# The mixer's values as one block of 1024 columns, with 7 products for three pairs

## The chip, the cores and the metric

The kernel runs on one core of a Trainium2 chip. The metric is the device time of one execution in microseconds (us). Five engines work side by side, each with its own queue of instructions in a fixed order, and wait for each other by semaphores: TensorE (PE in the profile, its weight loads PEld), VectorE (DVE), ScalarE (ACT), GpSimd (POOL) and SyncE (SP), which issues the transfers. TensorE reads its operands from SBUF and adds into PSUM.

## The reference

One layer of a streaming encoder over 256 frames of 2048 channels in f32: a SwiGLU feed-forward half step, a mixer, cross attention over 256 memory tokens, and a second feed-forward half step. Only the mixer is touched:

```python
h = rms_norm(x, mix_norm)
proj = h @ w_in                        # 2048 x 4112
u, q, k, v, g, a_lr = split(proj, [1024, 1536, 2048, 3072, 4096])
y_pool = pool_mixer(u, pool_w, pool_scale)     # 4 groups of 256 channels, a 256x256 map each
y_gla = gla_mixer(q, k, v, g, a_lr, ...)       # 4 heads, chunks of 64 frames
x = x + concat(y_pool, y_gla) @ w_out
```

So the columns of `w_in` are, in order, 1024 for the pool, 512 queries, 512 keys, 1024 values, 1024 gate and 16 for the decay. A head has 128 query and key columns and 256 value columns. In a head, decayed scores of queries and keys (zero above the chunk's end) weigh the values; the result is normed over its 256 channels, scaled by the norm's gain and multiplied by silu of the gate.

## The kernel before, in words

**Precision by splitting.** Each f32 operand of a large product is split into a high and a low half in a reduced format (fp32r), and three products stand for one: high by high, high by low, low by high. ScalarE casts the high half of a weight (`wh`, line 273), VectorE subtracts to get the low half (`wl`, line 274). The activations are kept split in `xs` and `ys`, tiles of 16 blocks of 128 channels, each with a high and a low half of 256 frames.

**The stream.** The class `Stream` holds the whole kernel as a list of units and operations. A unit is 1 MB of weights (2048 f32 on each of 128 partitions): a transfer into one of three `raw` buffers, a split into one of three `wh`/`wl` buffers, and the products on TensorE. `unit` appends one; `op(f, after)` appends other work behind the `after`th unit from there. On emission the splits run two units ahead of the products (`AHEAD = 2`), and the transfer of unit u + 3 is issued behind the split of unit u. The weight splits are held in their order on ScalarE and VectorE (`in_turn`), and `among_weights` puts other work at a place between them. Beyond that the framework's scheduler sets the order on each engine, by its own estimate of when things are ready. PSUM is a pool of four tiles of two banks each (`ptile`).

**Three forms of a product block.** `block_a` turns the product around (columns on partitions, 512 columns in 4 units of 32 matmuls). `block_b` has frames on partitions, 512 columns and 4 units of 24 matmuls into one PSUM tile. `block_s` has frames on partitions and 1024 columns, in 8 units of 2 channel blocks; a unit has 24 matmuls (`unit_p`), or, where it is listed as a pair in a `Sums` object, 7 products of half size by Strassen's scheme, 21 matmuls (`unit_s` and `seven`). Such a pair needs combinations of its four weight quarters (`split_seven`: T by three additions on line 457, then the split of T and of three of the quarters, `xh`/`xl`), combinations of the activations (`Sums.make`, lines 418 to 430, with a split), two more PSUM tiles (`open_parts`), and at the end additions that put the products together (`combine` and `join`, lines 542 to 557).

**The mixer.** In this order: two `block_a` for the pool's channels, whose evictions (`ev_pool`) write the pool's differences to `ys` blocks 8 to 15; the decay's 16 columns; `block_a` for queries and for keys; the pool's grouped product `pool_unit` from a unit of its own (`load_pool`), whose results `pool_out` writes to `ys` blocks 0 to 7 (lines 230 and 234); two `block_b` for the values, 512 columns each, evicted by ScalarE (`ev_v`) into the tile `v`; two `block_a` for the gate; then the output block. Among the units stand the heads' steps: `scores` scales the queries (lines 1102 and 1104), multiplies with the keys and copies the result to the one score tile `ST` (line 1118); `attend` multiplies `ST` and `v` (lines 1125 and 1128), squares on ScalarE (line 1134) and copies on VectorE (line 1136); `head_squares` adds (line 1140); `head_norms` sums over channels on TensorE (line 1147) and makes the root's reciprocal (lines 206 to 222) for two heads; `head_scale` spreads it (line 227) and scales. `ev_g` evicts a gate tile (lines 312, 313, 317), takes silu, multiplies, and splits into `ys` blocks 8 to 15.

The units of the values hold heads 0 and 1 in part: `scores(0)` comes after the first unit of the second values block, and the rest among its units and the first four gate units.

Of the kernel before, what the change touches and what calls it, by code (L numbers as in the profile page):

```python
# [7 lines left out]
F32 = mybir.dt.float32  # L8
F32R = mybir.dt.float32r
# [5 lines left out]
P = 128  # L15
# [78 lines left out]
def build(ctx, tc, I, out):  # L94
# [36 lines left out]
    def ptile(name):  # L131
        return psum.tile([P, 2, NB], F32, tag="ps", name=name)
# [6 lines left out]
    def uid(s):  # L139
        cnt[0] += 1  # L140
        return f"{s}{cnt[0]}"
# [256 lines left out]
    class Sums:  # L398
# [1 line left out]

        def __init__(self, name, act, pairs, over, room):
            self.name, self.act, self.pairs, self.over = name, act, pairs, over
            self.room, self.where = room, {}

        def make(self, g):
            act, i = self.act, self.pairs.index(g)
            n = 3 if self.over else 4
            if i == 0 or i >= self.room:  # L410
                room, tag = (self.room, self.name) if i == 0 else (1, f"{self.name}{i}")
                t = scope["pool"].tile([P, room * 6 * P], F32R, tag=tag, name=uid(tag))
                held = min(len(self.pairs), self.room) if i == 0 else 1
                t = t[:, : held * 2 * n * P].rearrange("p (g a n s) -> p g a n s", a=2, n=n, s=P)
                self.where.update({i + k: t[:, k] for k in range(held)})
            own = self.where[i]
            a, k = jtile(), slice(2 * g, 2 * g + 2)
            nc.vector.tensor_tensor(
                out=a.rearrange("p (k s) -> p k s", k=2), in0=f32(act[:, k, 0, :]),
                in1=f32(act[:, k, 1, :]), op=ALU.add,  # L420
            )

            a = a.rearrange("p (n s) -> p n s", n=4)
            p11, p21, p12, p22 = (a[:, m] for m in range(4))
            nc.vector.tensor_tensor(out=p11, in0=p11, in1=p21, op=ALU.subtract)
            nc.vector.tensor_tensor(out=p21, in0=p22, in1=p21, op=ALU.subtract)
            nc.vector.scalar_tensor_tensor(
                out=p22, in0=p11, scalar=-1.0, in1=p22, op0=ALU.mult, op1=ALU.subtract
            )
            added = nc.vector.tensor_tensor(out=p12, in0=p12, in1=p22, op=ALU.add)  # L430
            split(own[:, 0], own[:, 1], a[:, 4 - n :])
            if self.over:
                split(act[:, 2 * g, 0, P:], act[:, 2 * g, 1, P:], p11)
            return None, added
# [46 lines left out]
                    banks[n], x, w, start=n in fresh and j == 0, stop=n in ends and j == 2  # L481
                )

    def block_s(srcs, act, sums, order, evict, merge=None, sevens=None, late=0):

# [49 lines left out]

        def combine():

            e = held["e"] = scope["pool"].tile([P, 4, NB], F32, tag="sg", name=uid("sg"), bufs=2)  # L540
            a, b = held["parts"]
            nc.scalar.copy(e[:, 0], a[:, 0])
            nc.vector.tensor_tensor(out=e[:, 3], in0=a[:, 1], in1=e[:, 0], op=ALU.add)
            nc.vector.tensor_tensor(
                out=e[:, 1:3], in0=b, in1=e[:, 3:4].to_broadcast([P, 2, NB]), op=ALU.add
            )
            last = nc.vector.tensor_tensor(out=e[:, 3], in0=b[:, 1], in1=e[:, 1], op=ALU.add)
            if merge is not None:
                merge(e[:, 2:4], e[:, 0:2])
            return None, last  # L550
# [17 lines left out]
                st.unit(srcs[g], unit_p(g))  # L568
        for j in (1, 0):
            st.op(lambda j=j: join(j))  # L570

    def block_b(srcs, act, evict, delay=0):

        n_k = 4 * len(srcs)
        held = {}

        def unit(gi):
            def fn(wh, wl):
                if gi == 0:
                    held["ps"] = ptile(uid("pb"))  # L580
                wh, wl = (w.rearrange("p (k n) -> p k n", n=NB) for w in (wh, wl))
                for kk in range(4):
                    k = 4 * gi + kk
                    for h in range(2):
                        products(held["ps"][:, h, :], act, k, h, wh[:, kk], wl[:, kk],
                                 k == 0, k == n_k - 1)
            return fn

        for gi, src in enumerate(srcs):
            st.unit(src, unit(gi))  # L590
        st.op(lambda: evict(held["ps"]), delay)

    def wload(dst, w, k0, n, n0, cols=NB):
        nc.sync.dma_start(
# [301 lines left out]
    def down_first(wd, k0, nk, last, way):  # L896
# [3 lines left out]

    ffn(I["ffn1_w_gate"][0], I["ffn1_w_up"][0], I["ffn1_w_down"][0], down_first,
        amid_first)
    st.op(close_scope, 1)
    st.op(open_scope("s_mix"), 1)


    w_in = I["w_in"][0]
    mix = {}

    def mt(name, shape, tag=None, bufs=1):  # L910
        t = whole_lines(scope["pool"], shape, F32, tag or name, uid(name), bufs)
        mix[name] = t
        return t
# [149 lines left out]
    def ev_k(p, ps):  # L1063
# [3 lines left out]
        joined(ps, k)  # L1067
        nc.vector.tensor_tensor(out=k, in0=k, in1=mix["e"][:, 2 * p : 2 * p + 2, :], op=ALU.mult)

    block_a(wblock(w_in, 0), xs, ev_pool(0))  # L1070
    block_a(wblock(w_in, NB), xs, ev_pool(1))
    st.unit(load_a, a_unit, split_a)
    st.op(ev_a)
    st.op(decay, 2)
    block_a(wblock(w_in, 2 * NB), xs, ev_q)
    block_a(wblock(w_in, 3 * NB), xs, ev_k)
    st.unit(load_pool, pool_unit)
    for g in range(4):
        st.op(lambda g=g: pool_out(g))

    def ev_v(b):
        def evict(ps):
            if b == 0:
                mt("v", [P, 2, 2 * NB])
                s = mt("ST", [P, 2, S])
                nc.gpsimd.memset(s[64:128, 0, 0:CH], 0.0)
                nc.gpsimd.memset(s[64:128, 1, 2 * CH : 3 * CH], 0.0)
            for h in range(2):
                nc.scalar.activation(
                    mix["v"][:, h, b * NB : (b + 1) * NB], ps[:, h, :], AF.Copy, scale=Rcol[:, h : h + 1]  # L1090
                )
        return evict

    def scores(h):
        q, kd, E, F = mix["q"][:, h, :], mix["k"][:, h, :], mix["E"], mix["F"]
# [22 lines left out]
            nc.vector.tensor_copy(s[part, j // 2, j * CH :], ps[part, j // 2, j * CH : S])  # L1118

    def attend(h):  # L1120
        s, v = mix["ST"], mix["v"]
        po = ptile(uid("po"))
        for vt in range(2):
            col = h * DV + vt * P
            nc.tensor.matmul(
                po[:, vt, :S], v[:, 0, col : col + P], s[:, 0, :], start=True, stop=False
            )
            nc.tensor.matmul(
                po[:, vt, 2 * CH : S], v[:, 1, col : col + P], s[:, 1, 2 * CH :], start=False, stop=True
            )  # L1130
        if h % 2 == 0:
            mix["oz", h // 2] = as_four(m4())
        q = mix["osq", h] = ttile()
        nc.scalar.activation(q, po[:, :, :S], AF.Square)
        i = h % 2
        nc.vector.tensor_copy(mix["oz", h // 2][:, 2 * i : 2 * i + 2, :], po[:, :, :S])

    def head_squares(h):
        sq = mix["osq", h]
        nc.vector.tensor_tensor(out=sq[:, 0, :], in0=sq[:, 0, :], in1=sq[:, 1, :], op=ALU.add)  # L1140
# [14 lines left out]
    def head_scale(b):  # L1155
        ps = ptile(uid("ps"))
        for i in range(4):
            spread(ps[:, i // 2, :], i % 2, mix["diag"][i])
        for i in range(2):
            oz = mix["oz", b][:, 2 * i : 2 * i + 2, :]  # L1160
            nc.vector.tensor_tensor(out=oz, in0=oz, in1=bc(ps[:, i, :S]), op=ALU.mult)

    def ev_g(b):
# [10 lines left out]
            split_pair(ys, 8 + 2 * h, t)  # L1174
        return evict

    for b in range(2):
        block_b(wblock(w_in, (4 + b) * NB), xs, ev_v(b))
        for i in range(2):
            h = 2 * b + i  # L1180
            at = 1 + i - b
            st.op(lambda h=h: scores(h), at)
            st.op(lambda h=h: attend(h), at + 1)
            st.op(lambda h=h: head_squares(h), at + 1)
        st.op(lambda b=b: head_norms(b), 5 - 2 * b)
        st.op(lambda b=b: head_scale(b), 6 - b)
    block_a(wblock(w_in, 6 * NB), xs, ev_g(0), (0, 0))
    block_a(wblock(w_in, 7 * NB), xs, ev_g(1))
    st.op(close_scope, 1)
# [377 lines left out]
```

## Time and profile before

| | us |
|---|---|
| median of 3 runs | 2088.07 |
| lowest and highest | 2087.95, 2088.35 |
| the profiled execution | 2089.16 |
| its span, first to last instruction | 2087.4 |

| engine | busy us | share of the span |
|---|---|---|
| TensorE | 2074.1 | 99% |
| weight loads | 1728.9 | 83% |
| VectorE | 1791.1 | 86% |
| ScalarE | 1129.9 | 54% |
| POOL | 13.1 | 1% |

A row of a group gives line, engine, operation, what it writes and reads, shape and count, then busy time and mean duration of one in ns, then the idle time of the engine ahead of these instructions and what ended it. A row of the timeline gives start, duration, engine, line and operation. Matmuls are pipelined, so the mean duration of one (some 390 ns) is more than the distance from one to the next; the distance is read from a stretch's length and its count.

### The profile page before, as it was taken

How to read it: one execution, taken by the hardware profiler on the slowest of the kernel's cores; microseconds unless marked ns; L12 is line 12 of the kernel's file. 1: busy time of each engine (PE TensorE's matmuls, PEld its weight loads, DVE VectorE, ACT ScalarE, POOL GpSimd, SP SyncE). 2: the span in 40 equal slices, each digit the busy share in tenths (PEclk: the TensorE clock that was granted, in tenths of full speed). 3: DMA queues.
4: the chain of work that ended last, by engine and by line, in shares of the span. 5: the costliest groups of instructions: out<-in, count | busy, mean ns of one | idle time of the engine just before them, and what ended most of it. 6: DMA issues, size and time to landing. Idle time of an engine off the chain costs nothing.

```text
span 2087.4 us, 24205 instructions
## 1 busy us (share of the span) xinstructions
PE 2074.1 (99%) x9672; PEld 1728.9 (83%) x9672; DVE 1791.1 (86%) x1635; ACT 1129.9 (54%) x1116; POOL 13.1 (1%) x41
## 2 busy tenths in 40 slices
PE   9999999999999999999999999999999999999998
PEld 7888888888888888888888888888888888888886
DVE  7999899988998677678789777879998999989974
ACT  7655455644654545455755444556554555545544
POOL 0000000000000000000000000000000000000001
PEclk9999999999999999999999999999999999999999
DMA  7556666566656755457655455666576665676673
GB/s 263 202 196 228 241 222 205 191 230 223 237 191 238 240 166 183 160 187 266 230 183 183 160 182 181 213 211 205 178 242 216 237 209 184 226 239 222 209 255 118
DMA packets 131321, 435.94 MB, mean 209 GB/s; under 512 B 9860, under 2 KB 13544, under 8 KB 130824
## 3 DMA queue, kind: packets, MB, share of 16 engines
q1 hardware_dynamic: 131176, 434.38, 61.5%
q8 instruction: 76, 1.25, 0.2%
q14 instruction: 37, 0.30, 0.0%
q10 hardware_dynamic: 32, 0.01, 0.0%
HBM read 417.58 MB, written 16.78 MB: 208 GB/s over the span
## 4 chain that ended last, share of the span: by engine, by line
PE 96%; DVE 2%; issue 1%; ACT 0%; DMA 0%; SPq 0%; DVEq 0%
PE pt L356 55%; PE pt L480 25%; PE pa L341 6%; PE pe L356 3%; PE pb L356 2%; PE ph L747 1%; PE pl L1283 1%; PE pv L1322 1%; PE px L758 1%; DVE wl L461 0%; DVE T L457 0%; DVE xl L274 0%; DVE wl L274 0%; DMA x<-in_x 0%; PE pp L976 0%
## 5 line engine op out<-in xcount | busy, mean ns | idle before, releaser
L274 DVE TENSOR_TENSOR wl<-raw,wh 128x2048 fp32r<-128x2048 f32 (+2 forms) x268 | 600.5, 2248 | 166.4 <-ACT wh L273 165.6
L356 PE MATMUL pt<-wh,xs 128*128 128x512 f32 x2128 | 681.7, 390 | 0.5 <-ACT xs L230 0.5
L273 ACT CAST wh<-raw 128x2048 fp32r<-128x2048 f32 (+2 forms) x268 | 502.9, 1880 | 315.0 <-PE pt L356 136.8
L356 PEld LDWEIGHTS pt<-wh,xs 128*128 128x128 f32 x2128 | 398.3, 188 | 82.2 <-ACT xs L230 0.7
L460 ACT CAST wh<-T 128x1024 fp32r<-128x1024 f32 x228 | 239.8, 1054 | 364.2 <-DVE T L457 355.2
L356 PE MATMUL pt<-wh,ys 128*128 128x512 f32 x1360 | 428.3, 390 | 0.0
L356 PE MATMUL pt<-wl,xs 128*128 128x512 f32 x1064 | 415.6, 391 | 0.0
L356 PEld LDWEIGHTS pt<-wh,ys 128*128 128x128 f32 x1360 | 254.9, 188 | 52.5
L356 PE MATMUL pt<-wl,ys 128*128 128x512 f32 x680 | 264.9, 390 | 0.0
L461 DVE TENSOR_TENSOR wl<-T,wh 128x2048 fp32r<-128x2048 f32 x114 | 260.4, 2284 | 1.2 <-ACT wh L460 0.5
L356 PEld LDWEIGHTS pt<-wl,xs 128*128 128x128 f32 x1064 | 199.8, 188 | 41.2 <-DVE wl L274 0.2
L274 DVE TENSOR_TENSOR xl<-raw,xh 128x1536 fp32r<-128x1536 f32 x114 | 199.7, 1752 | 19.2 <-ACT xh L273 19.2
L273 ACT CAST xh<-raw 128x1536 fp32r<-128x1536 f32 x114 | 168.7, 1480 | 43.9 <-PE pt L480 28.7
L457 DVE TENSOR_TENSOR T<-T,raw 128x512 f32<-128x512 f32 x228 | 157.4, 690 | 6.1
L356 PEld LDWEIGHTS pt<-wl,ys 128*128 128x128 f32 x680 | 127.7, 188 | 26.3
L480 PE MATMUL pt<-wh,xs 128*128 128x512 f32 x364 | 141.8, 390 | 0.0
L457 DVE TENSOR_TENSOR T<-raw 128x1024 f32<-128x1024 f32 x114 | 138.9, 1219 | 1.6 <-DMA raw<-in_ffn_w_gate 1.1
L480 PE MATMUL pt<-xh,xs 128*128 128x512 f32 x364 | 136.7, 391 | 0.1
L341 PE MATMUL pa<-xs,wh 128*128 128x512 f32 x384 | 135.6, 397 | 0.0
L480 PE MATMUL pt<-wh,xe 128*128 128x512 f32 x320 | 124.5, 389 | 0.0
L341 PE MATMUL pa<-xs,wl 128*128 128x256 f32 x384 | 106.8, 282 | 0.0
L341 PEld LDWEIGHTS pa<-xs,wh 128*128 128x128 f32 x384 | 71.7, 188 | 16.4 <-issue 0.3
(238 smaller groups left out, 2286.2 us busy)
## 6 DMA issues: line engine op xcount, KB each, us to landing
raw<-in_ffn_w_down SPq DMA_DIRECT2D x88, 1024.0 KB, 5.5
raw<-in_ffn_w_up SPq DMA_DIRECT2D x80, 1024.0 KB, 5.0
raw<-in_ffn_w_gate SPq DMA_DIRECT2D x77, 1024.0 KB, 5.1
raw<-in_w_in SPq DMA_DIRECT2D x32, 1024.0 KB, 5.2
raw<-in_xattn_w_kv SPq DMA_DIRECT2D x32, 1024.0 KB, 5.1
raw<-in_w_out SPq DMA_DIRECT2D x16, 1024.0 KB, 5.5
raw<-in_xattn_w_q SPq DMA_DIRECT2D x16, 1024.0 KB, 5.6
raw<-in_xattn_w_o SPq DMA_DIRECT2D x16, 1024.0 KB, 5.5
```

The source lines that it names most:

```text
L273: in_turn("scalar", lambda: nc.scalar.copy(hi, src))
L274: in_turn("vector", lambda: nc.vector.tensor_tensor(out=lo, in0=src, in1=f32(hi), op=ALU.subtract))
L341: nc.tensor.matmul(o, w, x, start=k == 0 and i == 0, stop=last and i == 1)
L356: nc.tensor.matmul(ps, a, w, start=first and i == 0, stop=last and i == 2)
L457: in_turn("vector", lambda: nc.vector.tensor_tensor(out=o, in0=a, in1=b, op=ALU.add))
L460: in_turn("scalar", lambda: nc.scalar.copy(th[:, c], t[:, c]))
L461: in_turn("vector", lambda: nc.vector.tensor_tensor(out=tl, in0=t, in1=f32(th), op=ALU.subtract))
L480: nc.tensor.matmul(banks[n], x, w, start=n in fresh and j == 0, stop=n in ends and j == 2)
L747: nc.tensor.transpose(v[:, i, h * P : (h + 1) * P], g[:, h, i * P : (i + 1) * P], ident)
L758: nc.tensor.transpose(v[:, j, h * P : (h + 1) * P], x[:, h, j * P : (j + 1) * P], ident)
L1283: nc.tensor.matmul(ps[:, t, :M], ys[:, 4 * h + d, a, tok], xa["K", h][:, d, b, :], start=i == 0, stop=i == 11,)
L1322: nc.tensor.matmul(ps[:, d, :S], xa["V", h][:, m, a, col], xa["PT", h][:, m, b, :], start=i == 0, stop=i == 5,)
```

## The change

- The values become one `block_s` of 1024 columns. Pairs 1, 4 and 6 of its 8 units are done with 7 products; the combinations of the activations are kept in `ys` blocks 8 to 15 (`place`), free once the pooled product has read them. The mixer's scope gets single buffers for `T`, `xh` and `xl` (`MIX_HOMES`), and the tile `v` becomes two tiles' worth of a four-part tile that holds the joined products (`v_tile`). `ev_v` now scales in place, a head pair at a time.
- `block_b` is gone.
- The pool's grouped product stands ahead of the keys' block, not behind it.
- The sums of the activations are made one per unit, from the first key unit on.
- `scores(0)` is listed behind the sixth unit from the values' start; the heads follow the values, one per unit; `head_norms` and `head_scale` come 3 and 4 units, and 6 and 7 units, behind the values.
- The score tile `ST` shares the place of the decay's weights, and its zeros are written before the keys.

```diff
-        def __init__(self, name, act, pairs, over, room):
+        def __init__(self, name, act, pairs, over, room, place=None):
             self.name, self.act, self.pairs, self.over = name, act, pairs, over
-            self.room, self.where = room, {}
+            self.room, self.where, self.place = room, {}, place
...
-                t = scope["pool"].tile([P, room * 6 * P], F32R, tag=tag, name=uid(tag))
+                if self.place is not None:
+                    t = self.place
+                else:
+                    t = scope["pool"].tile([P, room * 6 * P], F32R, tag=tag, name=uid(tag))
...
-            e = held["e"] = scope["pool"].tile([P, 4, NB], F32, tag="sg", name=uid("sg"), bufs=2)
+            e = held["e"] = home()
...
+    MIX_HOMES = {"xh": [("xh", 3 * NB, 1)], "xl": [("xl", 3 * NB, 1)]}
     st.op(close_scope, 1)
-    st.op(open_scope("s_mix"), 1)
+    st.op(open_scope("s_mix", MIX_HOMES), 1)
...
+    V_PAIRS, V_ORDER = (1, 4, 6), (0, 1, 2, 3, 4, 5, 6, 7)
...
+    def score_tile():
+        t = mt("ST", [P, 2, S], tag="wa2")
+        nc.gpsimd.memset(t[64:128, 0, 0:CH], 0.0)
+        nc.gpsimd.memset(t[64:128, 1, 2 * CH : 3 * CH], 0.0)
+
+    def v_tile():
+        return scope["pool"].tile([P, 4, NB], F32, tag="v", name=uid("v"))
+
+    def ev_v(j, c):
+
+        mix["v", j] = c
+        for t in range(2):
+            nc.scalar.activation(c[:, t, :], c[:, t, :], AF.Copy, scale=Rcol[:, t : t + 1])
...
     block_a(wblock(w_in, 2 * NB), xs, ev_q)
-    block_a(wblock(w_in, 3 * NB), xs, ev_k)
     st.unit(load_pool, pool_unit)
     for g in range(4):
         st.op(lambda g=g: pool_out(g))
...
+    v_sums = Sums("", xs, V_PAIRS, False, len(V_PAIRS), ys[:, 8:].rearrange("p k a s -> p (k a s)"))
+    st.op(score_tile, 1)
+    for i, g in enumerate(V_PAIRS):
+        st.op(lambda g=g: among_weights(lambda: v_sums.make(g)), 1 + i)
+    block_a(wblock(w_in, 3 * NB), xs, ev_k)
...
-        s, v = mix["ST"], mix["v"]
+        s, v = mix["ST"], mix["v", h // 2]
...
-            col = h * DV + vt * P
+            col = h % 2 * DV + vt * P
...
+    st.op(lambda: scores(0), 6)
+    block_s(wwide(w_in, 4 * NB), xs, v_sums, V_ORDER, ev_v, home=v_tile)
+    for h in range(H):
+        st.op(lambda h=h: attend(h), 1 + h)
+        st.op(lambda h=h: head_squares(h), 1 + h)
+        if h + 1 < H:
+            st.op(lambda h=h: scores(h + 1), 1 + h)
     for b in range(2):
-        block_b(wblock(w_in, (4 + b) * NB), xs, ev_v(b))
-        for i in range(2):
-            h = 2 * b + i
-            at = 1 + i - b
-            st.op(lambda h=h: scores(h), at)
-            st.op(lambda h=h: attend(h), at + 1)
-            st.op(lambda h=h: head_squares(h), at + 1)
-        st.op(lambda b=b: head_norms(b), 5 - 2 * b)
-        st.op(lambda b=b: head_scale(b), 6 - b)
+        st.op(lambda b=b: head_norms(b), 3 + 3 * b)
+        st.op(lambda b=b: head_scale(b), 4 + 3 * b)
     block_a(wblock(w_in, 6 * NB), xs, ev_g(0), (0, 0))
```

More of the change, by code (lines that the diff above doesn't have):

```diff
@@ L482, in seven, with parts_tile, block_s @@
                 )
-    def block_s(srcs, act, sums, order, evict, merge=None, sevens=None, late=0):
+    def parts_tile():
+        return scope["pool"].tile([P, 4, NB], F32, tag="sg", name=uid("sg"), bufs=2)
+    def block_s(srcs, act, sums, order, evict, merge=None, sevens=None, late=0, home=parts_tile):
         sevens = [g for g in order if g in (sevens or sums.pairs)]
@@ L570, in block_s @@
             st.op(lambda j=j: join(j))
[L572 to L591, printed above, removed]
     def wload(dst, w, k0, n, n0, cols=NB):
@@ L1079, in build @@
         st.op(lambda g=g: pool_out(g))
[L1081 to L1092, printed above, removed]
+    v_sums = Sums("", xs, V_PAIRS, False, len(V_PAIRS), ys[:, 8:].rearrange("p k a s -> p (k a s)"))
[3 more added lines that the diff above has]
+    block_a(wblock(w_in, 3 * NB), xs, ev_k)
     def scores(h):
```

## The prediction

> **What bounds the kernel now.** I read the page first, then the sums by stretch of time around the mixer, then groups by form, then the timelines of VectorE and ScalarE. From the page, parts 1 and 4:
>
> ```profile
> span 2087.4 us, 24205 instructions
> PE 2074.1 (99%) x9672; PEld 1728.9 (83%) x9672; DVE 1791.1 (86%) x1635; ACT 1129.9 (54%) x1116; POOL 13.1 (1%) x41
> PE 96%; DVE 2%; issue 1%; ACT 0%; DMA 0%; SPq 0%; DVEq 0%
> ```
>
> TensorE is the path: a matmul less is time gained, and any microsecond in which TensorE waits is lost. The stretches that the change touches (values, then heads and gate; below them the values alone, the keys and the pooled product by their tiles). Columns: stretch, its length, busy time and instructions of TensorE, its weight loads, VectorE, ScalarE and POOL (an engine with none is left out), then the granted clock:
>
> ```profile
> 812.63:861.87 49.24, 49.24 (x235) 39.93 (x233) 27.21 (x38) 22.61 (x27) 0.00 (x0) 1.00 0.58 189
> 861.87:913.91 52.04, 52.04 (x316) 45.82 (x314) 35.56 (x60) 24.41 (x26) 0.00 (x0) 1.00 0.44 145
> ```
> ```profile
> 812.63:839.95 27.32, 27.32 (x120) 22.34 (x120) 1.27 (x2) 1.00 0.59 191
> ```
> ```profile
> 784.38:806.89 22.51, 22.51 (x129) 19.42 (x127) 1.37 (x2) 1.65 (x3) 1.00 0.54 182
> ```
> ```profile
> 806.89:812.63 5.74, 5.74 (x48) 5.69 (x47) 0.47 (x1) 0.47 (x1) 1.00 0.62 210
> ```
>
> The first two columns are equal in every row: TensorE is never idle here. A values matmul takes 27.32 / 120 = 0.228, one of the keys or the gate 22.51 / 128 = 0.176 (a wide and a narrow one alternate). VectorE is at 27.21 of 49.24 in the values; its idle time before the weight splits of this whole stretch is
>
> ```profile
> L274 DVE TENSOR_TENSOR wl<-raw,wh 128x2048 fp32r<-128x2048 f32 x16 | 36.7, 2291 | 28.1 <-ACT wh L273 28.0
> ```
>
> **Matmuls removed.** The values go from 2 x 4 units of 24 products (192) to 5 units of 24 and 3 pairs of 7 x 3 (183). 9 x 0.228 = 2.05 gained, all on the path. That is the whole possible gain: 0.1%, while about 0.2% (4.2 us) is what a measurement of this kernel can tell from no change.
>
> **The pooled product ahead of the keys.** Its 48 matmuls and the keys' 128 are the same in either order (28.25 together), so the values again start 28.25 after the queries' end (784.38), at 812.63. Its load moves past four key loads on SP's queue, and each of these goes one place later:
>
> ```profile
> raw<-in_w_in SPq DMA_DIRECT2D x32, 1024.0 KB, 5.2
> raw<-in_pool_w SPq DMA_DIRECT2D x1, 1024.0 KB, 5.4
> ```
>
> Equal sizes, 5.2 to 5.4 to land, three buffers ahead: taken at nothing, covered by the two units (over 11 us) between a load and its use; without that cover it would be some 5. The two memsets of the score tile move back on POOL, 1% busy: nothing. The eight evictions of the pooled product (a ScalarE and a VectorE half each) now fall into the keys; that matters below.
>
> **VectorE's new work and where it queues.** A unit with 7 products needs, beside the same splits, these:
>
> ```profile
> L461 DVE TENSOR_TENSOR wl<-T,wh 128x2048 fp32r<-128x2048 f32 x114 | 260.4, 2284 | 1.2 <-ACT wh L460 0.5
> L274 DVE TENSOR_TENSOR xl<-raw,xh 128x1536 fp32r<-128x1536 f32 x114 | 199.7, 1752 | 19.2 <-ACT xh L273 19.2
> L457 DVE TENSOR_TENSOR T<-T,raw 128x512 f32<-128x512 f32 x228 | 157.4, 690 | 6.1
> L457 DVE TENSOR_TENSOR T<-raw 128x1024 f32<-128x1024 f32 x114 | 138.9, 1219 | 1.6 <-DMA raw<-in_ffn_w_gate 1.1
> ```
>
> so 1.22 + 2 x 0.69 + 1.75 + 2.28 = 6.63 of VectorE against 2.29 of a plain unit, while TensorE needs only 21 x 0.228 = 4.8. Ahead of it come three sums of the activations (L418 to L430 and a split of 512 columns, nearest row PT's), and the evictions of pool and keys:
>
> ```profile
> L418 DVE TENSOR_TENSOR j<-xs 128x512 f32<-128x512 f32 x12 | 8.2, 682 | 0.0
> L425 DVE TENSOR_TENSOR j<-j 128x128 f32<-128x128 f32 x25 | 7.2, 289 | 0.6
> L280 DVE TENSOR_TENSOR PT<-pt,PT 128x512 fp32r<-128x512 f32 x4 | 2.6, 683 | 0.0
> L234 DVE SCALAR_TENSOR_TENSOR ys<-pp,gains,ys 128x256 fp32r<-128x256 f32 x8 | 3.7, 480 | 0.7 <-ACT ys L230 0.7
> L313 DVE TENSOR_TENSOR k<-pa,c 128x512 f32<-128x512 f32 x2 | 1.4, 688 | 1.4 <-ACT c L312 1.4
> ```
>
> A sum is 0.68 + 4 x 0.29 + 0.68 = 2.52, three 7.6. With 3 x 4.3 more for the pairs and 5.0 for recombining (five additions of T's sizes: 2 x 0.69 + 3 x 1.22), VectorE gets 25.6 more, nearly the 28.1 that it has idle. The question is where. Up to here VectorE's queue of the two kernels has the same times, in the stretch after the queries:
>
> ```profile
> 793.52 0.69 DVE L313 TENSOR_TENSOR q<-pa,c 128x512 f32<-128x512 f32 x1
> 794.76 0.68 DVE L1059 SCALAR_TENSOR_TENSOR q<-q,R 128x512 f32<-128x512 f32 x1
> 795.37 2.38 DVE L1052 TENSOR_TENSOR F<-F,E 128x4 f32<-128x4 f32 x1
> 797.66 2.28 DVE L274 TENSOR_TENSOR wl<-raw,wh 128x2048 fp32r<-128x2048 f32 x1
> ```
> ```profile
> 794.91 2.81 POOL L1045 TENSOR_TENSOR m<-m,R 128x1024 f32<-128x1024 f32 x1 [32.37 <-ACT m L1044]
> ```
>
> The changed kernel's order of instructions on VectorE puts, from 797.66 to the low half that the first pair's second product reads (xl of the second values unit): three plain splits (6.84), three scalings of q (0.75), six pool evictions (2.88), the three sums (7.56), T (2.60), four instructions on the keys (2.76), xl (1.75): 25.1. (The keys' second PSUM tile is the queries': its join above ends at 794.2, and TensorE's order touches that tile after 30 key products, at 784.38 + 5.74 + 30 x 0.176 = 795.4: no wait.) Neighbours overlap by 0.09 (795.37 + 2.38 against 797.66) where the next does not read the last, at about 24 of 38 places: -2.1. Twice it waits for ScalarE, which in turn waits for a VectorE half of the pool's evictions (the cast of the last key unit now stands behind one): about +1.0. So xl is ready at 821.7. TensorE wants it 28 matmuls after the values' start: 812.63 + 28 x 0.228 = 819.0. **It waits 2.7**, and 0.1 more for the low half of T behind it: 2.8. If all 38 overlap and no ScalarE wait occurs, 0.4; with no overlap, 4.8. I take 2.8, worked from the order as it stands. After that VectorE is ahead again (two plain splits against two units of 5.5), and the later pairs, whose single xh and xl buffers come free after the first 9 products, have over 2 to spare.
>
> [...]
>
> **The heads behind the values.** Four heads now lie between the gate's first four units, one per unit, where before two lay in the values. The matmuls are the same, but their order on TensorE is not: after the last product of the fourth gate unit (call it G) come, with no gate product between them, attend of head 2, scores of head 3, the norms of heads 0 and 1, attend of head 3, the spread of these norms, and only then gate unit five, whose PSUM tile is free only when VectorE has joined the first gate tile. VectorE and ScalarE rows of before for these steps, and the TensorE time of scores, attend, half a norm, spread, with VectorE's copies of a score tile last:
>
> ```profile
> 877.06:877.85 0.79, 0.79 (x9) 0.59 (x9) 0.43 (x1) 0.32 (x1) 0.00 (x0) 1.00 0.00 0
> 884.41:885.72 1.31, 1.31 (x10) 1.20 (x8) 0.86 (x1) 0.42 (x1) 0.00 (x0) 1.00 0.04 13
> 885.72:886.08 0.36, 0.36 (x6) 0.36 (x5) 0.36 (x1) 0.16 (x1) 0.00 (x0) 1.00 0.00 0
> 878.66:879.47 0.81, 0.81 (x10) 0.81 (x8) 0.81 (x1) 0.00 (x0) 0.00 (x0) 1.00 0.00 0
> 857.79:859.18 1.39, 1.39 (x6) 1.11 (x7) 1.29 (x4) 0.00 (x0) 0.00 (x0) 1.00 0.31 41
> ```
> ```profile
> 871.89 0.69 DVE L1136 COPY m<-po 128x512 f32<-128x512 f32 x1
> 872.49 0.42 DVE L1140 TENSOR_TENSOR t<-t 128x256 f32<-128x256 f32 x1
> 872.83 0.25 DVE L1104 TENSOR_SCALAR m<-q,E 128x64 f32<-128x64 f32 x1
> ...
> 873.64 0.25 DVE L1104 TENSOR_SCALAR m<-q,E 128x64 f32<-128x64 f32 x1
> 873.83 0.18 DVE L210 RECIPROCAL r<-chain 128x4 f32<-128x4 f32 x1
> ...
> 874.65 0.88 DVE L222 TENSOR_SCALAR diag<-ident,r 128x128 f32<-128x128 f32 x4
> ```
> ```profile
> 889.65 1.29 ACT L312 COPY c<-pa 128x512 f32<-128x512 f32 x2 [3.14 <-PE pa L341]
> 890.84 1.91 ACT L273 CAST wh<-raw 128x2048 fp32r<-128x2048 f32 x1
> 892.76 1.28 ACT L1168 ACT_TABLE_LOAD   x1
> ```
> ```profile
> L1134 ACT ACTIVATE t<-po 128x512 f32<-128x512 f32 x4 | 2.4, 599 | 2.8 <-PE po L1128 2.8
> ```
>
> From G: ScalarE copies the second gate half (0.6), casts gate unit seven (1.91, ahead in its queue), then squares head 2 (0.60): G + 3.1. VectorE copies head 2 and sums (0.69 + 0.42), then scales q for head 3 (six, 872.83 to 873.89, 1.06): the first three by G + 4.7, all by G + 5.1. TensorE's scores of head 3 begin, two norm halves (0.72), the rest of the scores: G + 6.2. On VectorE the root's reciprocal comes ahead of the score copies: G + 6.4, copies (1.39) G + 7.8. Attend of head 3 ends G + 8.6; the norm's factors (from the end of L210 at 874.01 to the last diagonal at 875.53, 1.5) are done at G + 9.3, the spread G + 9.6, the join (0.69) G + 10.0. TensorE's own work in it is 1.31 + 0.79 + 0.72 + 1.31 + 0.81 = 4.9, **so 5.1 of waiting**. Without the cast in the way it is 3.1 (the cast takes 1.9); with the table load, here hidden under VectorE's scalings, exposed and a second 0.6 copy behind G, 6.9. I take 5.1. Behind it gate units five to eight (22.5) cover both gate evictions and the last norms, and the output block's own waits stay as they are.
>
> **Sum.** -2.05 + 2.8 + 5.1 = +5.8. The profiled execution, 2089.16 against the median of 2088.07, goes to 2095.0; the median to 2093.9.
>
> **Rivals.**
> - First pair hidden, heads not: VectorE overlaps more than I count, its lower end being 0.4. Price -2.05 + 5.1 = +3.0: 2091.1. Against it: 25 us of queue in the 21.3 between 797.66 and 819.0.
> - Heads hidden, first pair not: 2088.07 - 2.05 + 2.8 = 2088.8. Against it: no gate product stands in that part of TensorE's order.
> - Nothing waits: only the 9 matmuls count, 2086.0, not slower. It decides if the xl of the first pair is in place by 819.0 and head 2's square does not wait for the cast. For it: before, the same kinds of chain were covered without loss (both stretches above are full).
> - Both at their upper ends: -2.05 + 4.8 + 6.9 = +9.7: 2097.7.
> [...]
>
> **How the numbers follow.** Forecast 0.48, first pair hidden 0.15, heads hidden 0.08, nothing waits 0.12, both at the upper end 0.10, clock 0.07. The prediction is the forecast's 2093.9, whose own range (first pair 1.5 to 4, heads 4 to 6) is 2091.5 to 2096. From 2088.5 to 2098 only "nothing waits" and small tails are out. Slower by over 0.2% (above 2092.2): 0.48 + 0.10 + 0.07 = 0.65; within: 0.15 + 0.08 + 0.10 = 0.33; faster 0.02, the tail of "nothing waits".
>
> **What will show it.** Right: a TensorE gap of about 3 before an L480 product with xl some 6 after the values begin, ended by VectorE xl L274; a run of waits of about 5 among scores, attend and norms after the fourth gate unit, ended by ScalarE and VectorE of the heads; 183 values products. Wrong: either stretch with TensorE's columns equal, a granted clock under 1.00 there, or a wait in the output block that before did not have.

## The result, and the profile after

The changed kernel takes 2098.72 us (median of 4 runs; 2097.56 to 2100.69); the kernel before, run beside it, 2088.21 (2087.95 to 2088.63). The ratio is 1.005, 95% interval 1.0038 to 1.0062: slower by 10.5 us, where 5.8 was forecast. The profiled execution takes 2098.07. From its page, the span, the busy times and the chain of work that ended last:

```profile
span 2096.3 us, 24240 instructions
PE 2077.4 (99%) x9663; PEld 1731.5 (83%) x9663; DVE 1814.3 (87%) x1670; ACT 1137.1 (54%) x1126; POOL 12.6 (1%) x41
PE 94%; DVE 4%; ACT 1%; issue 1%; DMA 0%; SPq 0%; DVEq 0%
```

TensorE has its 9 matmuls less (9663 against 9672) and is still busy for 3.3 us more, and VectorE has 4% of the chain where it had 2%. The sums by stretch of time place it (columns as in the prediction: length, TensorE, its weight loads, VectorE, ScalarE, POOL, then the granted clock, which is the share of TensorE's full clock). The rows are the values up to the first scores, the gate up to G (the end of gate unit four, here 886.12), the heads' chain behind G up to gate unit five (898.55), and, without their first 4.4 us, the other four gate units:

```profile
811.90:857.78 45.88, 43.21 (x184) 35.06 (x182) 40.42 (x36) 22.11 (x18) 0.00 (x0) 0.96 0.62 206
857.78:886.12 28.34, 28.34 (x171) 24.17 (x170) 18.74 (x34) 12.66 (x17) 0.00 (x0) 1.00 0.53 172
886.12:898.55 12.43, 8.13 (x41) 6.84 (x40) 6.40 (x24) 5.47 (x10) 0.00 (x0) 0.77 0.09 34
902.95:923.44 20.49, 20.49 (x124) 18.03 (x123) 15.37 (x21) 8.92 (x9) 0.00 (x0) 1.00 0.51 164
```

Before, the values and the gate were full and at clock 1.00. Now the values have 2.67 idle and a clock of 0.96, the chain 4.30 idle and a clock of 0.77; the other two rows are full and at 1.00. From the start of the values to the end of the gate it is 111.54 (811.90 to 923.44) against 101.28 before (812.63 to 913.91), 10.3 more, where the whole span grew by 8.9: the loss lies here, whole. The 9 matmuls should have made it 99.2, so 12.3 were added, of which idle time is only 6.97.

TensorE's timeline in the two places (start, duration, then in brackets the idle time ahead and what ended it):

```profile
821.10 0.80 PE L483 MATMUL pt<-xl,xs 128*128 128x512 f32 x1 [2.67 <-DVE xl L274]
821.69 0.63 PE L483 MATMUL pt<-xh,xs 128*128 128x512 f32 x1
822.12 0.63 PE L483 MATMUL pt<-wh,ys 128*128 128x512 f32 x1
...
890.89 0.62 PE L1106 MATMUL pq<-m,k 128*64 128x256 f32 x2 [3.31 <-DVE m L1098]
...
894.29 1.19 PE L1119 MATMUL po<-ST,v 128*128 128x256 f32 x2 [0.99 <-DVE ST L1112]
```

Both waits are where the prediction put them, ended by what it named. The rows behind the first show the part that was missed: the matmuls start 0.43 apart (821.69, 822.12), not 0.228. The sums by stretch again, cut at the borders at which the granted clock changes; they lie on a grid of 3.413 us (from 821.03 to 892.71 it is 71.68, 21 times that):

```profile
817.62:821.03 3.41, 0.81 (x4) 0.34 (x2) 3.41 (x5) 1.62 (x2) 0.00 (x0) 1.00 0.00 0
821.03:824.44 3.41, 3.34 (x8) 2.67 (x9) 3.41 (x3) 3.03 (x2) 0.00 (x0) 0.50 0.64 187
...
885.88:889.29 3.41, 1.71 (x11) 1.37 (x9) 0.06 (x1) 3.30 (x6) 0.00 (x0) 1.00 0.36 144
889.29:892.71 3.42, 1.82 (x14) 1.43 (x15) 2.11 (x9) 1.61 (x4) 0.00 (x0) 1.00 0.00 0
892.71:896.12 3.41, 2.42 (x11) 1.91 (x8) 2.73 (x12) 0.20 (x1) 0.00 (x0) 0.50 0.02 5
896.12:899.53 3.41, 3.41 (x15) 3.21 (x14) 2.48 (x6) 0.60 (x1) 0.00 (x0) 0.50 0.00 0
```

Three stretches of 3.41 us have the clock at 0.50, one behind the first wait and two behind the heads'. In them TensorE is busy for 3.34 + 2.42 + 3.41 = 9.17 us, half of which, 4.6, full clock would have saved. With the 6.97 idle that is 11.6 of the 12.3; 0.7 is not placed.

### The profile page after: what moved, and what is told of

It is laid out like the page before. It is cut to its first block, busy times and chain, and to the rows that moved or that the text cites. A ratio compares the mean times of both kernels' runs of the same rounds, so it can differ in the third digit from the quotient of the medians.

```text
span 2096.3 us, 24240 instructions
## 1 busy us (share of the span) xinstructions
PE 2077.4 (99%) x9663; PEld 1731.5 (83%) x9663; DVE 1814.3 (87%) x1670; ACT 1137.1 (54%) x1126; POOL 12.6 (1%) x41
## 4 chain that ended last, share of the span: by engine, by line
PE 94%; DVE 4%; ACT 1%; issue 1%; DMA 0%; SPq 0%; DVEq 0%
PE pt L356 56%; PE pt L483 26%; PE pa L341 5%; PE pe L356 3%; PE ph L733 1%; DVE wl L274 1%; DVE T L460 1%; PE pl L1277 1%; PE pv L1316 1%; PE px L744 0%; DVE xl L274 0%; DVE wl L464 0%; ACT wh L273 0%; DMA x<-in_x 0%; PE pq L1106 0%
## 5 line engine op out<-in xcount | busy, mean ns | idle before, releaser
L274 DVE TENSOR_TENSOR wl<-raw,wh 128x2048 fp32r<-128x2048 f32 (+2 forms) x265 | 593.7, 2247 | 152.4 <-ACT wh L273 151.6
L356 PE MATMUL pt<-wh,xs 128*128 128x512 f32 x2208 | 707.3, 390 | 0.1
L273 ACT CAST wh<-raw 128x2048 fp32r<-128x2048 f32 (+2 forms) x265 | 497.0, 1880 | 305.5 <-PE pt L356 134.4
L356 PEld LDWEIGHTS pt<-wh,xs 128*128 128x128 f32 x2208 | 413.3, 188 | 85.0 <-ACT xs L230 0.4
L463 ACT CAST wh<-T 128x1024 fp32r<-128x1024 f32 x234 | 245.9, 1053 | 367.0 <-DVE T L460 360.6
L356 PE MATMUL pt<-wl,xs 128*128 128x512 f32 x1104 | 431.2, 391 | 0.0
L464 DVE TENSOR_TENSOR wl<-T,wh 128x2048 fp32r<-128x2048 f32 x117 | 267.3, 2284 | 1.3 <-ACT wh L463 0.5
L356 PEld LDWEIGHTS pt<-wl,xs 128*128 128x128 f32 x1104 | 207.3, 188 | 42.8
L274 DVE TENSOR_TENSOR xl<-raw,xh 128x1536 fp32r<-128x1536 f32 x117 | 204.9, 1751 | 21.3 <-ACT xh L273 21.3
L483 PE MATMUL pt<-wh,xs 128*128 128x512 f32 x370 | 144.2, 390 | 0.0
L483 PE MATMUL pt<-xh,xs 128*128 128x512 f32 x376 | 141.5, 392 | 0.1
```

The source lines that it names most:

```text
L273: in_turn("scalar", lambda: nc.scalar.copy(hi, src))
L274: in_turn("vector", lambda: nc.vector.tensor_tensor(out=lo, in0=src, in1=f32(hi), op=ALU.subtract))
L463: in_turn("scalar", lambda: nc.scalar.copy(th[:, c], t[:, c]))
L464: in_turn("vector", lambda: nc.vector.tensor_tensor(out=tl, in0=t, in1=f32(th), op=ALU.subtract))
L483: nc.tensor.matmul(banks[n], x, w, start=n in fresh and j == 0, stop=n in ends and j == 2)
```

## The experiments

The question was whether the half clock is an effect of the two waits, and whether the terms 2.8 and 5.1 are right without it. Each kernel is the changed kernel with the edit shown, except where another is named. The kernel before ran beside each group: 2088.01 beside the first four, 2088.33 beside the second four, 2088.24 beside the last two.

**The first pair one unit later.**

```diff
-    V_PAIRS, V_ORDER = (1, 4, 6), (0, 1, 2, 3, 4, 5, 6, 7)
+    V_PAIRS, V_ORDER = (2, 4, 6), (0, 1, 2, 3, 4, 5, 6, 7)
```

> The 7-product pairs are 2, 4 and 6 instead of 1, 4 and 6; nothing else. Theory of waits with the clock: the first pair comes one unit of 24 products (5.5 us) later, VectorE has its xl ready in time, so both the 2.8 us wait in the values and the half clock behind it (1.5 us) go: 4.3 less than the changed kernel's 2098.7, about 2094.4, with a granted clock of 1.00 over all the values. Rival, waits alone (the clock has another cause than the wait): the wait goes and the half clock stays, about 2095.9. Rival, VectorE is short over the whole block and not only ahead of the first pair: the wait only moves, 2098.7. The heads behind the fourth gate unit still take some 12.4 us.

Measured: 2093.62 (2093.14 to 2095.11), ratio 1.0027 (1.0017 to 1.0038): 5.1 less than the changed kernel. Sums by stretch of this kernel: the values, then a part of its heads' chain:

```profile
811.90:853.40 41.50, 41.50 (x185) 34.08 (x183) 39.67 (x35) 20.38 (x17) 0.00 (x0) 1.00 0.68 228
...
884.02:887.43 3.41, 1.30 (x9) 0.94 (x9) 2.00 (x8) 2.13 (x5) 0.00 (x0) 1.00 0.00 0
887.43:890.85 3.42, 2.43 (x11) 1.96 (x11) 1.84 (x8) 0.20 (x1) 0.00 (x0) 0.50 0.00 0
```

In the values both the idle time and the half clock are gone; VectorE, busy for 39.67 of 41.50, is nearly full there and yet late nowhere. It was short ahead of the first pair only. It remains 5.6 over before, so with the 2.05 saved some 7.7 are the heads', whose chain has its half clock as it was (887.43 to 894.26).

**The heads one unit earlier.** Then this with the pairs 2, 4 and 6 together.

```diff
-    for h in range(H):
-        st.op(lambda h=h: attend(h), 1 + h)
-        st.op(lambda h=h: head_squares(h), 1 + h)
+    for h, at in enumerate((0, 1, 2, 3)):
+        st.op(lambda h=h: attend(h), at)
+        st.op(lambda h=h: head_squares(h), at)
         if h + 1 < H:
-            st.op(lambda h=h: scores(h + 1), 1 + h)
+            st.op(lambda h=h: scores(h + 1), at)
     for b in range(2):
-        st.op(lambda b=b: head_norms(b), 3 + 3 * b)
-        st.op(lambda b=b: head_scale(b), 4 + 3 * b)
+        st.op(lambda b=b: head_norms(b), (2, 5)[b])
+        st.op(lambda b=b: head_scale(b), (3, 6)[b])
```

> Each head is one unit earlier (head h at 0 + h units behind the values, the norms at 2 and 5, the factors at 3 and 6), so that gate products stand between most of the heads' steps on TensorE; the values with the pairs 1, 4 and 6 are left as they are. Theory of waits with the clock: the heads' 7.5 us (5.0 of waits, 2.5 of half clock) go, less up to 2 us for the first attend, which now comes straight behind the values: 2091.2 to 2093.2, with the half clock only in the values. Rival, waits alone: 5.1 go, 2093.6 to 2095.6, and a clock under 1.00 stays around the heads. Rival, the heads' chain is too long for any place among the gate units: the waits come back in other places, 2096 or more.

> Both edits together: pairs 2, 4 and 6, and the heads one unit earlier. Theory of waits with the clock: the values cost -2.05 (9 matmuls) and nothing else, the heads up to 2 us for the first attend, a granted clock of 1.00 throughout: 2086.1 to 2088.2, not slower than before. Rival, waits alone: what of the clock is not tied to the two waits stays, some 2.7 us more: 2088.9 to 2090.9.

Measured: 2100.23 (ratio 1.0058, 1.0043 to 1.0073) and 2093.68 (1.0026, 1.0016 to 1.0037). Neither came as expected; the second was to be no slower than before. TensorE's waits longer than 1 us from the first attend on, in the first kernel and then in the second:

```profile
863.23 1.19 PE L1119 MATMUL po<-ST,v 128*128 128x256 f32 x2 [3.93 <-ACT v L1070]
868.46 0.62 PE L1106 MATMUL pq<-m,k 128*64 128x256 f32 x2 [2.32 <-DVE m L1098]
```
```profile
857.48 0.67 PE L1119 MATMUL po<-ST,v 128*128 128x256 f32 x2 [3.09 <-ACT v L1070]
862.33 1.08 PE L1106 MATMUL pq<-m,k 128*64 128x256 f32 x2 [2.33 <-DVE m L1098]
```

The chain behind G no longer waits, but the first attend stands straight behind the last values product and waits 3.1 to 3.9 for ScalarE to scale `v`, and the next scores 2.3 for VectorE, with half clock behind both (862.88 to 866.29 and 869.70 to 873.12 in the first kernel, 858.25 to 868.49 in the second). I had allowed 2 for this. The rival that the waits only change place was right for this edit.

**The clock alone: idle work in the two waits.** Transposes of the identity into PSUM columns that are overwritten or never read: 12 behind the first product of the values' first pair, 15 ahead of head 3's scores.

```diff
-    def seven(banks, act, sums, g, fresh, ends, weights, order):
+    def seven(banks, act, sums, g, fresh, ends, weights, order, fill=0):
...
+                if n == "P1" and j == 0:
+                    for _ in range(fill):
+                        nc.tensor.transpose(banks["P6"][:, :P], ident, ident)
...
-                seven(held["banks"], act, sums, g, fresh, ends, weights, order)
+                seven(held["banks"], act, sums, g, fresh, ends, weights, order,
+                      fill if g == sevens[0] else 0)
...
         ps = ptile(uid("pq"))
+        for _ in range(15 if h == 3 else 0):
+            nc.tensor.transpose(ps[:, 0, S : S + P], ident, ident)
...
-    block_s(wwide(w_in, 4 * NB), xs, v_sums, V_ORDER, ev_v, home=v_tile)
+    block_s(wwide(w_in, 4 * NB), xs, v_sums, V_ORDER, ev_v, home=v_tile, fill=12)
```

> The changed kernel with idle work for TensorE in its two longest waits: 12 transposes of the identity (0.21 us each, 2.5 in all) behind the first product of the first pair, and 15 (3.2 us) ahead of head 3's scores, into PSUM columns that are overwritten or never read. No wait is taken away. Theory of waits with the clock: the granted clock stays at 1.00 in both places, the first products behind each wait take 0.228 and not 0.427 us: 1.5 less in the values and some 2.5 less in the heads, about 2094.7. Rival (the half clock comes with the load, not with standing still): the clock falls all the same and the time is 2098.7 or some tenths more, for transposes that run longer than the wait.

Measured: 2093.99 (2093.13 to 2095.24), ratio 1.0028 (1.0018 to 1.0038): 4.7 less than the changed kernel, with 27 matmuls more. TensorE's timeline in the values, then the sums by stretch behind the first wait and of the heads' chain:

```profile
819.07 1.47 PE L488 MATMUL pt<-ident 128*128 128x128 f32 x12
...
822.08 0.50 PE L483 MATMUL pt<-xl,xs 128*128 128x512 f32 x1 [1.30 <-DVE xl L274]
```
```profile
821.50:828.00 6.50, 5.92 (x25) 4.67 (x26) 6.50 (x4) 4.48 (x3) 0.00 (x0) 1.00 0.57 173
886.00:896.20 10.20, 8.28 (x60) 7.26 (x59) 6.64 (x25) 5.35 (x9) 0.00 (x0) 1.00 0.08 31
```

A transpose took 0.12 us (12 in 1.47) and not the 0.21 I had reckoned with, which is what the 16 at the start of the kernel before took (3.4 in all), so about half of each wait stayed idle. That was enough: the clock is 1.00 in both places, and xl still comes 2.8 late (1.47 + 1.30). Here the half clock follows from the standing still (2.67 and 3.31 without the transposes, 1.30 and 0.75 with them), not from the load, which is the same behind both.

Not all of the 4.7 is the clock's. Among the heads the transposes also moved the norms of heads 0 and 1 ahead of head 3's first score products, behind two of which they stood, and so into the wait: the norms begin at 889.62 and the scores at 890.60, where in the changed kernel it is 891.44 and 890.89. Transposes and idle time are 3.7 there, where the changed kernel waits 4.3. From the first values product to the output block the traces have 106.52 against 111.54: 5.0 less, some 0.5 of it shorter waits, which leaves 4.5 for the clock. That is near the 4.6 that the three stretches gave.

**Half the idle work:** 6 and 8 transposes in the same places.

> As the filled kernel, with half the idle work: 6 transposes (1.3 us) in the wait of the values and 8 (1.7 us) ahead of head 3's scores, so that TensorE still stands still for 1.4 and 1.6 us. The records of the clock so far show half clock in stretches of 3.413 us that lie on one grid of that length, each behind a stretch of the grid in which TensorE was busy 0.53 or less of the time. By that (share of the grid's stretch): about 0.6 busy is enough, full clock, the same 2094.0 as the filled kernel. Rival (any stand-still of over about 1 us brings the half clock): 2096 to 2098.7.

Measured: 2095.77 (2093.55 to 2096.89), ratio 1.0033 (1.0021 to 1.0044), between the two expectations. Sums by stretch of its profiled execution (2095.0), cut on the grid of its clock:

```profile
817.77:821.18 3.41, 1.71 (x11) 1.23 (x9) 3.41 (x5) 1.40 (x2) 0.00 (x0) 1.00 0.00 0
821.18:824.60 3.42, 3.13 (x13) 2.41 (x14) 3.42 (x3) 3.25 (x2) 0.00 (x0) 1.00 0.55 162
...
889.45:892.86 3.41, 2.07 (x17) 1.72 (x17) 2.94 (x16) 0.72 (x2) 0.00 (x0) 1.00 0.00 0
892.86:896.28 3.42, 3.42 (x16) 3.24 (x16) 2.35 (x8) 0.60 (x1) 0.00 (x0) 0.50 0.02 5
```

In the values the stretch with 1.71 busy is followed by full clock; among the heads one with 2.07 busy is followed by half clock. The busy share alone, by which I had forecast, does not decide it. This is one execution; of the other five, four took 2095.56 to 2096.89 and one 2093.55.

**The heads over all eight gate units,** with the pairs 2, 4 and 6. `mix["wide"]` is a tile in the place of `xl`, free by then; `gated` is what `ev_g` did behind `joined`, for the first gate block one unit later.

```diff
-            t = ttile()
+            if b == 0 and p == 0:
+                mix["wide"] = scope["pool"].tile([P, 3 * NB], F32R, tag="xl", name=uid("xl"), bufs=1)
+            if b == 0:
+                t = f32(mix["wide"][:, p * NB : (p + 1) * NB]).rearrange("p (a b) -> p a b", a=2)
+            else:
+                t = ttile()
+            mix["t", h] = t
             joined(ps, t, rows["R"], b == 0)
+            if b == 1:
+                gated(b, p)
+        return evict
+
+    def gated(b, p):
...
-        st.op(lambda h=h: attend(h), 1 + h)
-        st.op(lambda h=h: head_squares(h), 1 + h)
+        st.op(lambda h=h: attend(h), (1, 2, 4, 5)[h])
+        st.op(lambda h=h: head_squares(h), (1, 2, 4, 5)[h])
         if h + 1 < H:
-            st.op(lambda h=h: scores(h + 1), 1 + h)
+            st.op(lambda h=h: scores(h + 1), (1, 3, 5)[h])
     for b in range(2):
-        st.op(lambda b=b: head_norms(b), 3 + 3 * b)
-        st.op(lambda b=b: head_scale(b), 4 + 3 * b)
+        st.op(lambda b=b: head_norms(b), (3, 6)[b])
+        st.op(lambda b=b: head_scale(b), (5, 7)[b])
     block_a(wblock(w_in, 6 * NB), xs, ev_g(0), (0, 0))
+    for p in range(2):
+        st.op(lambda p=p: gated(0, p), 1)
```

> Pairs 2, 4 and 6, and the heads over all eight gate units: attend of heads 0 to 3 after units 1, 2, 4 and 5, the next head's scores after units 1, 3 and 5, the norms after 3 and 6, the factors after 5 and 7; the first gate's SiLU, its product with the heads and its split come one unit behind its join, so that the gate's PSUM tile is free without the norms. On TensorE at least 17 gate products (3 us) then stand between each two steps of which one waits for the other. Theory (VectorE's work for the heads is hidden where gate products stand in between, and without waits the clock stays): -2.05 and nothing else, about 2086, granted clock 1.00 throughout. Rival, VectorE and ScalarE have no room for the heads among the gate's splits at any spacing: 2 to 5 us of waits stay, 2088 to 2091.

Measured: 2086.12 (2085.74 to 2086.66), ratio 0.9988 (0.9979 to 0.9998): 2.2 less than before and 12.6 less than the changed kernel. It beats both, the kernel before by about what the 9 matmuls are worth, with an interval that ends just below 1. Its trace bears the gain out: from the first values product to the output block it takes 98.90, where the kernel before takes 101.28. Sums by stretch: the values but for their first 0.5 us, and 150 us around the whole change:

```profile
811.90:853.02 41.12, 41.12 (x183) 33.78 (x181) 39.29 (x35) 20.20 (x17) 0.00 (x0) 1.00 0.70 230
...
800.00:950.00 150.00, 150.00 (x773) 126.32 (x772) 127.97 (x178) 81.53 (x85) 0.00 (x0) 1.00 0.60 196
```

TensorE is never idle and the clock is 1.00. VectorE and ScalarE do the same work as in the changed kernel; what is new is that gate products stand between the steps and that the first gate's SiLU comes later. The run does not tell these two apart.

**The pool's product behind the keys again.** The sums of the activations then overwrite `ys` blocks 8 to 15 before the pool has read them, so the pooled branch works on other numbers; the amount of work is the same.

```diff
-    st.unit(load_pool, pool_unit)
-    for g in range(4):
-        st.op(lambda g=g: pool_out(g))
...
     block_a(wblock(w_in, 3 * NB), xs, ev_k)
+    st.unit(load_pool, pool_unit)
+    for g in range(4):
+        st.op(lambda g=g: pool_out(g))
```

> One part undone: the pool's grouped product stands behind the keys again, all else as in the changed kernel. Theory (VectorE's queue ahead of the first pair is as long in either order, so its place does not matter): the wait ahead of the first pair's xl stays at 2.5 to 3, 2098.7 within 1.5. Rival (with the product sooner, its eight evictions are out of the way by the values; behind the keys they meet the first pair): up to 2.9 us more of wait (6 halves of 0.48), 2100 to 2102.

Measured: 2100.43 (2098.54 to 2101.10), ratio 1.0053 (1.0038 to 1.0068); the intervals do not tell it from the changed kernel. But my theory said that the wait stays ahead of the first pair, and it does not. TensorE's timeline at the first values product:

```profile
812.14 0.51 PE L356 MATMUL pt<-wh,xs 128*128 128x512 f32 x1 [2.54 <-DVE k L313]
```

The pressure on VectorE shows itself sooner: the keys' join is late, and the first values product waits for its PSUM tile. Half of the pooled product then stands among the first pair's products (819.33 to 821.73 on TensorE), so TensorE takes xl only at 822.31, and VectorE has it ready at 818.14. In all, four stretches have half clock: one behind the 2.54, and three among the heads, where the eight norm products take 1.87 (1.05 in the changed kernel). The mean granted clock of the profiled execution is 0.995, where the changed kernel has 0.996.

**The pool's product sooner, alone:** the kernel before with `load_pool`, `pool_unit` and `pool_out` ahead of the keys.

> One part alone: the kernel before, with the pool's grouped product ahead of the keys and nothing else. Theory: the same matmuls in another order, loads three buffers ahead: no difference, within 0.5 of before. Rival (VectorE now evicts the pool among the keys' splits and is late for the keys or the decay): TensorE idle ahead of a key unit, 1 to 3 us more.

Measured: 2088.31 beside 2088.33, ratio 0.9999 (0.999 to 1.0008). As expected, it costs nothing by itself.

**The two terms, each by itself at full clock.** For the heads: pairs 2, 4 and 6, with the 15 transposes ahead of head 3's scores. For the values: the heads over eight gate units, with the first pair at 1 and the 12 transposes in its wait.

> The kernel with pairs 2, 4 and 6 and the heads as in the changed kernel, with the 15 transposes ahead of head 3's scores: only the waits of the heads are left, without the values' wait and without the half clock. This prices one term of the prediction's sum: before - 2.05 + 5.1, 2091.2 within 0.7. Rival (the waits of the heads are worth 6 or more and the clock less): 2092 or more.

> The kernel with the heads over all eight gate units, with the first pair back at 1 and the 12 transposes in its wait: only the wait ahead of the first pair is left, without the heads' waits and without the half clock. This prices the other term: before - 2.05 + 2.8, 2088.9 within 0.7. Rival (the wait alone is worth 4.3, the clock nothing): 2090.4.

Measured: the heads' waits alone 2090.22 (2089.55 to 2091.47; ratio 1.0009, 1.0000 to 1.0018), the values' wait alone 2089.25 (2088.57 to 2089.93; ratio 1.0004, 0.9995 to 1.0013). Over the 2.05 less for the matmuls that is 2.0 + 2.05 = 4.0 for the heads (5.1 expected) and 1.0 + 2.05 = 3.1 for the values (2.8 expected). TensorE's timeline among the heads of the first; then the stretch from the first values product to the first gate product, in the second and in the kernel with the heads over eight gate units, which has no wait there:

```profile
883.42 1.80 PE L1109 MATMUL pq<-ident 128*128 128x128 f32 x15
...
885.98 1.05 PE L1148 MATMUL pn<-ones,t 128*128 128x1 f32 x8 [0.75 <-DVE m L1137]
...
888.86 0.67 PE L1126 MATMUL po<-ST,v 128*128 128x256 f32 x2 [1.02 <-DVE ST L1119]
```
```profile
811.65:857.25 45.60, 44.29 (x205) 36.08 (x203) 41.36 (x37) 22.03 (x18) 0.00 (x0) 1.00 0.63 208
```
```profile
811.43:853.81 42.38, 42.38 (x192) 34.76 (x190) 40.55 (x35) 21.36 (x19) 0.00 (x0) 1.00 0.68 223
```

The values take 45.60 against 42.38 without the wait: 3.2. Among the heads, transposes and idle time are 1.80 + 0.75 + 1.02, and 0.15 ahead of gate unit five: 3.7. As in the filled kernel the norms stand ahead of the scores here and use part of the wait, so the 4.0 is not the price of the changed kernel's own order.

## Why the prediction was wrong

**The matmuls, -2.05: right.** With all waits gone the kernel is 2.2 under before (2.4 in the traces).

**The first pair, +2.8: right in place and cause, 0.3 to 0.4 short in size.** The queue ahead of xl was reckoned to end at 821.7, with 2.7 of wait. VectorE's timeline of the changed kernel:

```profile
819.29 1.75 DVE L274 TENSOR_TENSOR xl<-raw,xh 128x1536 fp32r<-128x1536 f32 x1
```

It ends at 821.04; TensorE's values began 0.7 sooner too, and it waited 2.67. From the split at 797.43 on, the queue took 23.6, where 24.0 was reckoned; that the waits agree to 0.03 is luck. The plain sum of VectorE's idle time in the stretch did not show this wait. The queue in its order did, and the later pair, which needs the same work and waits for nothing, bears it out.

**The heads, +5.1: right in place and in what ended the first wait; the size is not settled.** ScalarE and VectorE behind G (886.12):

```profile
886.80 1.90 ACT L273 CAST wh<-raw 128x2048 fp32r<-128x2048 f32 x1
888.60 0.60 ACT L1128 ACTIVATE t<-po 128x512 f32<-128x512 f32 x1
```
```profile
889.23 0.69 DVE L1130 COPY m<-po 128x512 f32<-128x512 f32 x1 [4.40 <-ACT t L1128]
```

The square stands behind the cast as forecast, and the scores began at G + 4.8 (4.7 forecast). By the prediction's own times TensorE waits some 3.4 there, 1.1 ahead of the last attend, and 0.6 behind it, for the norms' factors and the join. In the changed kernel it was 3.31, 0.99 and nothing. But the half clock lengthened the steps between, and the only runs at full clock have the norms in another place, with 4.0 in all. No run has this chain at full clock in the order that the prediction reckoned with.

**What the sum lacked: the clock.** No term of the sum is for the clock, and no row of before that the prediction shows has it under 1.00. The prediction gives the clock a chance of its own, 0.07, beside the forecast's 0.48, though the forecast itself had TensorE standing still for 2.7 in the values and for 3.4 behind G. Measured, both waits brought half clock: 4.6 us by the busy time of the three stretches, 4.7 by the idle work, 5.5 by the difference between the changed kernel's 10.5 and the terms taken singly (-2.05 + 3.1 + 4.0). The last two hold the other place of the norms too. The forecast's 5.8 and the 4.6 make 10.4, against 10.5 measured. The filled kernel's 2093.99 lies at the forecast's 2093.9 partly by luck: its heads wait less than the 5.1, and its time is 0.9 more than the three terms taken singly give. The range ended at 2098.0 because the clock was added to no other case: waits and clock were separate chances in the prediction, but are one chain of cause in the kernel. A granted clock under 1.00 in these stretches was among the signs of being wrong that it named.

The kernel before does show half clock, at its end, where TensorE has done its last product. Sums by stretch of its profile, on the grid of its clock:

```profile
2076.40:2079.82 3.42, 1.36 (x6) 0.78 (x5) 2.35 (x6) 2.77 (x9) 1.76 (x2) 1.00 0.34 124
2079.82:2083.23 3.41, 0.00 (x0) 0.00 (x0) 2.28 (x6) 1.38 (x3) 0.00 (x0) 0.50 0.71 256
```

TensorE stood still for only some 2 of the 3.41 us of the first of them (1.36 busy), and half clock followed. So the trace of before already had half clock behind a stretch that was idle only in part, and by it a wait of 2.7 that falls within one stretch could have been expected to bring it.

**The grid of the clock, and the queue ahead of the split.** The trace of the changed kernel has the clock at 0.50 for 3.413 us from 821.03, at 1.00 for 68.267, then at 0.50 for 6.827 from 892.71: 1, 20 and 2 times 3.413. The wait of 2.67, the shorter of the two, was enough to bring half clock. Ahead of the split at 797.43 (797.66 before), where the prediction's queue begins, VectorE's timeline of the changed kernel has two instructions in the other order:

```profile
794.80 2.31 DVE L1047 SCALAR_TENSOR_TENSOR q<-q,R 128x512 f32<-128x512 f32 x1
797.03 0.15 DVE L1040 TENSOR_TENSOR F<-F,E 128x4 f32<-128x4 f32 x1
```

Of the two, the first that starts after POOL's instruction has begun (at 794.91 before, 794.16 here) is the long one in both kernels: 2.31 and 0.15 here, where it was 0.68 and 2.38. Together they took 2.46, where it was 3.06. No run shows why.

## What to carry to other kernels

On an engine that is never idle, price a new wait by its length and by what the clock does behind it: here waits of 2.7 and 4.3 us cost some 4.6 us more by half clock. Look for half clock in the whole trace of the kernel before, its end too, before you leave it out of a sum. A saving of 2 us on the engine at the bound is only had if its own work stands between the steps that wait for other engines: with 17 products or more between the heads' steps, the first gate's SiLU later and the first pair one unit later, nearly the same instructions turned +10.5 into -2.2. And idle work put into a wait is a cheap way to tell the clock's share of a loss from the wait's, if one reads from the trace whether the order of the other work has moved with it.

## What the runs showed of the hardware

The borders of half clock lie on a grid of 3.413 us in the traces of the kernel before and the changed kernel. A stretch of the grid need not be idle to bring half clock: TensorE was busy for 0.81 of 3.41 us ahead of one at half clock, for 1.30 in another kernel, and for 1.82 ahead of the heads'. In the rows of six kernels (the one before at its end, the changed one, the pair later, the heads earlier, both, half the idle work) every stretch at full clock with 0.00 to 1.36 busy was followed by half clock. Between 1.71 and 2.07 both occurred: 1.71, in two kernels, and 1.89 were followed by full clock, 1.82 and 2.07 by half. Half clock went on behind stretches at half clock with 1.75, 2.42, 2.43 and 2.74 busy, and it ended behind those with 2.90, 3.34, 3.41 and 3.42. So busy time alone does not sort the cases, and no run shows what does.

Runs of one kernel differ in time and granted clock together: with the first pair one unit later, the five runs of 2093.14 to 2093.77 had a mean granted clock of 0.997, the three of 2094.46 to 2095.11 had 0.996.
